# A reordered opening and 128-row attention scores in a two-layer streaming encoder

## The chip, the cores and the metric

The kernel runs on one core of a Trainium2 chip. The metric is the time of one execution on the device in microseconds. Engines in the rows: PE is TensorE (matmuls), PEld its weight loads, DVE is VectorE, ACT is ScalarE, POOL is GpSimd and SP is the engine whose queue issues nearly all DMAs.

## What is computed

512 frames of width 1024 pass through two layers; all data is float32.

```python
h = rms_norm(x, ev_norm_g)                       # layer 0
z = h @ w_in                                     # 1024 -> 2560: u_a, gate_a, val_b, glu_b, gate_b
y_a = s5_mixer(u_a, ...) * silu(gate_a)          # 32 groups of 16 channels, 64 complex states each
y_b = conv_module(val_b, glu_b, ...) * silu(gate_b)   # GLU, causal depthwise conv of 31 taps, LayerNorm, SiLU
x = x + concat(y_a, y_b) @ w_out
x = x + mem_cross_attention(rms_norm(x), mem_n, ...)  # 4 heads, 256 memory tokens
h = rms_norm(x, od_norm_g)                       # layer 1
q, k, v, g = split(h @ w_in, 4)                  # 16 heads of 64
s = q @ k.T * scale + bias                       # chunks of 64; each sees itself and 8 before it
x = x + (softmax(s) @ v * silu(g)) @ w_out
x = x + mem_cross_attention(rms_norm(x), mem_n, ...)
return rms_norm(x, final_norm_g)
```

`s5_mixer` discretises a diagonal complex system (exp, sine and cosine of the parameters), runs it as a scan over the frames, and ends in a GELU and a gated linear unit (GLU).

## The kernel before

Activations stand channel-major: eight tiles of 128 channels x 512 frames. Precision is kept by splitting each f32 operand into a rounded high half and a low half; a projection tile `proj` of 128 output channels is 24 matmuls of 512 columns (high x high, high x low, low x high over eight input tiles). Its weights come through `weights`: DMA into `raw` (three buffers), high half on ScalarE into `whi` (two buffers), low half by a subtraction on GpSimd or, if asked, VectorE into `wlo` (three buffers). The result goes to a PSUM buffer `proj`, of which there are three.

The scheduler orders each engine's queue from the traced order, priorities and its own model of times; what is marked `pinned` stays behind what was traced before it on its engine. Each queue then runs in that order.

Layer 0 begins with loads and splits written out by hand (`LOADS`, `ACTS`): ScalarE makes high halves of `h`, squares for the norm follow, VectorE makes low halves and adds the squares. TensorE warms up, runs the first two tiles (u0, u1) as the tiles of x come in (`first_mm`), then tile w12 in parts, with the row sums (`st0.done`, four one-column f32 matmuls) pinned between its first twelve matmuls and the rest. `rsqrt` on VectorE turns the sums into the norm, a matmul broadcasts it over the partitions, and ScalarE copies it to `rb0`: every tile's result is multiplied by `rb0` as it leaves PSUM.

`s5_tables` follows: some 150 small VectorE operations that make the discretised system and the rotation tables. Then the stage runs in the order of `PLAN`; each letter is a step for tile or slice i:

- u: S5 input tile (`state_input`), with a round trip through DRAM. c: gate tile and value tile of the conv (`conv_input`). v: the conv as 40 small f32 matmuls (`conv_taps`). g: a gate tile.
- a, b, o: the S5 slice's tables (`s5_prep`), scan (`s5_scan`) and output (`s5_output`); y then goes through DRAM. The slices share the tiles `w`, `M` and `hh`.
- m, n: squares and sums of the memory. l, s: LayerNorm of the conv.

After the plan come the Gelu of each slice, the GLU's 16 f32 matmuls (line 891), the keys and values of the memory, the output projection, the first cross-attention, the chunk attention and the second cross-attention.

In the chunk attention, head pairs run through `score`, softmax, `transposed` and `weigh` with a written order, every matmul pinned; projection matmuls of later head pairs (`Filler`) lie between. A head's scores are two products: the tile `q` holds high and low half on 64 rows each, and the key's high half stands twice, so the first product has 128 rows; the second, q's high half with the key's low half, takes the 64 rows of that head:

```python
r = slice(64 * (hd % 2), 64 * (hd % 2) + 64)
terms=((q, k[hd % 2]), (q[r], k[2][r]))
```

Of the kernel before, what the change touches and what calls it, by code (L numbers as in the profile page):

```python
# [44 lines left out]
def kernel(  # L45
# [22 lines left out]
    V, A, G, T = nc.vector, nc.scalar, nc.gpsimd, nc.tensor  # L68
# [133 lines left out]
    class Stats:  # L202
# [13 lines left out]
        def done(self, scale=1.0 / D, pin=False):  # L216
            nb = self.n // P
            ps = psum("acc")
            for b in range(nb):
                c = slice(b * P, (b + 1) * P)  # L220
                ins = T.matmul(ps[:, b:b + 1], self.acc[:, c], ones[:, 0:1], start=True, stop=(self.late is None))
                if pin:
                    pinned(ins)
# [47 lines left out]
    def s5_tables(l0):  # L271
# [13 lines left out]
        def exp16(out, a):  # L285
            a = ts(slot(), a, -87.33, 88.37, ALU.max, ALU.min)
# [60 lines left out]
        run(exp16(dt, pc("log_dt")))  # L347
# [109 lines left out]
        cp = l0.tile([P, 2, NPAIR, 32], F32, name="cp")  # L457
        pinned(G.memset(cp, 0.0))
# [17 lines left out]
        w = [l0.tile([P, 4, 4, 32], F32, name=f"w{e}") for e in range(4)]  # L476
        M = l0.tile([P, 4, 4, 32], F32, name="M")
        for t in w + [M]:
            pinned(G.memset(t, 0.0))
        hh = [l0.tile([P, 4, NJ], F32, name=f"hh{e}") for e in range(2)]  # L480
        d3 = l0.tile([P, 4, NJ], F32, name="d3")
        for t in hh + [d3]:
            pinned(G.memset(t[:, :, 0:1], 0.0))
        return dict(pr=pr[:, :, 1:5], npi=npi, apr=ap[0], api=ap[1], rot=rot, far=ang[:, 8], m4=m4,
                    bb=wide(bb), cz=wide(cz), cp=cp, w=w, M=M, hh=hh, d3=d3)
# [40 lines left out]
    def s5_scan(tb, sl, U, prep):  # L526
# [13 lines left out]
        powers(qs, tb["pr"], tb["npi"], tb["cz"], w2r, w2i, ALU.add, ALU.subtract, True, G, "g")  # L540
# [148 lines left out]
    N12 = 12  # L689
    WLO = 'VVVV'  # L690
# [21 lines left out]
    with tc.high_priority():  # L712
        for job in ACTS.split():
            n = int(job[1])
            if job[0] == "x":
                ins = A.activation(h0[n][0], x[n], AF.Copy, scale=pc("ev_g", n))
                stt(h0[n][1], x[n], pc("ev_g", n), f(h0[n][0]), ALU.mult, ALU.subtract)
# [9 lines left out]
            else:  # L727
                c = slice(0, 4) if job[0] == "a" else slice(4, 8)
                ins = A.copy(his[job], raws[n][:, c])
                tt(los[n][:, c], raws[n][:, c], f(his[job]), ALU.subtract,  # L730
                   {"G": G, "V": V}[WLO[2 * (job[0] == "b") + n]])
            pinned(ins)
# [20 lines left out]
    w12 = weights(w_in_d[12])  # L753
    ps12 = psum("proj")
    mm12 = [(w12[i][:, k], h0[k][j]) for i, j in ((0, 0), (0, 1), (1, 0)) for k in range(KT)]

    def run12(lo, hi, pin=False):
        for n in range(lo, hi):
            ins = T.matmul(ps12, mm12[n][0], mm12[n][1], start=(n == 0), stop=(n == len(mm12) - 1))
            if pin:  # L760
                pinned(ins)
# [10 lines left out]
    def conv_input(i):  # L772
        ps = proj(weights(w_in_d[12 + i], eng=V if UENG[4 + 2 * i] == "V" else G), h0) if i else ps12
# [4 lines left out]
        ps = proj(weights(w_in_d[8 + i], eng=V if UENG[5 + 2 * i] == "V" else G), h0)  # L778
# [725 lines left out]
```

## Time and profile before

| | us |
|---|---|
| median of three runs (1022.0, 1023.16, 1024.18) | 1023.16 |
| profiled execution | 1018.19 |
| its span, first to last instruction | 1016.4 |
| TensorE busy in the span | 975.5 |
| VectorE, ScalarE, GpSimd busy | 565.1, 467.3, 453.1 |
| mean granted TensorE clock, of full speed | 0.979 |

Times in rows are microseconds from the start of the span. Busy time of TensorE counts a pipelined matmul from its start to a modelled end, so records overlap; the distance from one start to the next is what a matmul takes in a run of them. Each f32 matmul stands as two records. "idle before <-releaser" is what the engine waited for.

### The profile page before, as it was taken

The numbers are of one execution on the slowest core, as the hardware profiler recorded it, in microseconds if no ns is written. First come the engines' busy times: TensorE is split into PE (matmuls) and PEld (weight loads), VectorE is DVE, ScalarE is ACT, GpSimd is POOL, SyncE is SP. The second block draws the span as 40 slices with busy tenths as digits, with TensorE's granted clock in tenths as the row PEclk, the third lists the DMA queues.
The fourth block names the chain that finished last, engine by engine and source line by source line (L and its number), as shares of the span: only waits on it lengthen the run. The fifth ranks groups of instructions, "written<-read, shape, count | busy, mean of one in ns | idle before, by whom it ended". The sixth has DMA issues, their size and how long they took to land.

```text
span 1016.4 us, 14244 instructions
## 1 busy us (share of the span) xinstructions
PE 975.5 (96%) x5336; PEld 825.6 (81%) x5336; DVE 565.1 (56%) x1249; ACT 467.3 (46%) x844; POOL 453.1 (45%) x252
## 2 busy tenths in 40 slices
PE   8979999998999999999999999999999999999996
PEld 6768998867978888888778787787878898888895
DVE  8895665454144433353477677767667412333476
ACT  6223444364444433344355555556645543333352
POOL 2530332016857434437443345335426885344242
PEclk9987999999999999999999999999999999999998
DMA  7455556535532222223222122221213453222153
GB/s 256 134 149 174 152 173 188 156 104 185 189 124 84 83 83 65 80 68 109 84 77 69 63 94 70 76 68 68 75 62 109 143 183 116 84 83 63 62 165 106
DMA packets 53620, 113.71 MB, mean 112 GB/s; under 512 B 13232, under 2 KB 24624, under 8 KB 53552
## 3 DMA queue, kind: packets, MB, share of 16 engines
q1 hardware_dynamic: 53408, 112.74, 34.9%
q8 instruction: 42, 0.69, 0.3%
q14 instruction: 26, 0.21, 0.1%
q10 hardware_dynamic: 144, 0.07, 0.0%
HBM read 106.50 MB, written 6.29 MB: 111 GB/s over the span
## 4 chain that ended last, share of the span: by engine, by line
PE 38%; DVE 7%; issue 2%; ACT 2%; POOL 1%; DMA 1%; POOLq 0%; ACTq 0%; DVEq 0%
PE ps_proj L978 20%; PE ps_proj L175 4%; PE ps_proj L1170 3%; PE ps_proj L630 2%; PE ps_att L1213 2%; PE ps_tr L1243 2%; PE ps_att L1040 1%; PE ps_acc L1256 1%; PE ps_tr L1256 1%; DVE h L139 1%; ACT whi L150 1%; DVE pe L144 1%; POOL wlo L135 1%; DVE o L135 1%; DVE tz L144 1%
## 5 line engine op out<-in xcount | busy, mean ns | idle before, releaser
L135 POOL TENSOR_TENSOR wlo<-raw,whi 128x1024 fp32r<-128x1024 f32 x133 | 322.2, 2425 | 416.0 <-ACT whi L150 394.0
L150 ACT CAST whi<-raw 128x1024 fp32r<-128x1024 f32 x148 | 154.9, 1048 | 194.4 <-issue 52.5
L978 PE MATMUL ps_proj<-h,whi 128*128 128x512 f32 x896 | 228.6, 398 | 0.0
L978 PEld LDWEIGHTS ps_proj<-h,whi 128*128 128x128 f32 x896 | 164.3, 189 | 36.8 <-issue 4.1
L978 PE MATMUL ps_proj<-h,wlo 128*128 128x512 f32 x448 | 115.6, 397 | 0.0
L175 PE MATMUL ps_proj<-og,whi 128*128 128x512 f32 (+1 forms) x576 | 109.8, 340 | 0.6 <-DVE og L135 0.6
L175 PEld LDWEIGHTS ps_proj<-og,whi 128*128 128x128 f32 x576 | 90.0, 188 | 14.3 <-DVE og L135 2.0
L978 PEld LDWEIGHTS ps_proj<-h,wlo 128*128 128x128 f32 x448 | 85.0, 191 | 18.4 <-issue 0.2
L175 PE MATMUL ps_proj<-h,whi 128*128 128x512 f32 x272 | 71.6, 410 | 1.6 <-ACT whi L150 1.6
L175 PEld LDWEIGHTS ps_proj<-h,whi 128*128 128x128 f32 x272 | 51.5, 195 | 13.4 <-ACT whi L150 2.1
L135 DVE TENSOR_TENSOR pt<-ps_tr,pt 128x512 fp32r<-128x512 f32 (+1 forms) x80 | 39.9, 525 | 33.0 <-ACT pt L150 32.8
L175 PE MATMUL ps_proj<-og,wlo 128*128 128x512 f32 (+1 forms) x288 | 57.9, 338 | 0.0
L150 ACT CAST pt<-ps_tr 128x512 fp32r<-128x512 f32 (+1 forms) x80 | 34.2, 460 | 46.8 <-PE ps_tr L1243 28.2
L139 DVE SCALAR_TENSOR_TENSOR h<-x,par,h 128x512 fp32r<-128x512 f32 x32 | 47.0, 1474 | 13.5 <-ACT h L229 13.5
L1222 ACT ACTIVATE pe<-ps_att,s 128x128 f32<-128x128 f32 (+3 forms) x64 | 33.5, 525 | 39.4 <-DVE s L144 34.3
L135 POOL TENSOR_TENSOR sa<-sa,sq 128x512 f32<-128x512 f32 (+1 forms) x28 | 39.0, 1392 | 27.5 <-ACT sq L210 27.3
L175 PEld LDWEIGHTS ps_proj<-og,wlo 128*128 128x128 f32 x288 | 45.7, 188 | 6.4 <-POOL wlo L135 0.2
L144 DVE TENSOR_SCALAR pe<-pe,s 128x256 f32<-128x256 f32 (+3 forms) x96 | 50.0, 543 | 1.4
L135 DVE TENSOR_TENSOR kv<-ps_proj,kv 128x256 fp32r<-128x256 f32 (+1 forms) x24 | 12.2, 510 | 68.8 <-ACT kv L150 68.8
L794 PEld LDWEIGHTS ps_proj<-x,cw 128*128 128x128 f32 x320 | 44.3, 215 | 6.0 <-DVE uu L135 3.5
L794 PE MATMUL ps_proj<-x,cw 128*128 128x64 f32 (+4 forms) x320 | 45.0, 297 | 3.8 <-DVE uu L135 3.1
L135 DVE TENSOR_TENSOR z<-ps_proj,rb 128x512 f32<-128x512 f32 x32 | 22.0, 687 | 47.2 <-PE ps_proj L978 47.1
(256 smaller groups left out, 1643.3 us busy)
## 6 DMA issues: line engine op xcount, KB each, us to landing
raw<-in_xa_qg_dram SPq DMA_DIRECT2D x32, 512.0 KB, 3.5
raw<-in_od_qkg_dram SPq DMA_DIRECT2D x24, 512.0 KB, 3.5
raw<-in_xa_o_dram SPq DMA_DIRECT2D x22, 512.0 KB, 3.5
cw<-in_cw_dram SPq DMA_DIRECT2D x32, 320.0 KB, 3.1
raw<-in_w_in_dram SPq DMA_DIRECT2D x18, 512.0 KB, 4.0
raw<-in_xa_k_dram SPq DMA_DIRECT2D x16, 512.0 KB, 3.5
raw<-in_xa_v_dram SPq DMA_DIRECT2D x16, 512.0 KB, 3.5
x<-in_xT_dram SPq DMA_DIRECT2D x16, 256.0 KB, 4.6
```

Source lines behind the costliest of these rows:

```text
L135: (eng or V).tensor_tensor(out, a, b, op=op)
L139: V.scalar_tensor_tensor(out=out, in0=a, scalar=s, in1=b, op0=op0, op1=op1)
L144: V.tensor_scalar(out=out, in0=in0, scalar1=s1, scalar2=None, op0=op0)
L150: A.copy(hi, src)
L175: T.matmul(ps, a, b, start=(i == 0), stop=(i == len(prods) - 1))
L630: T.matmul(o, a[:, ts_], b[:, k, :], start=(e == 0 and low == 0 and t % 2 == 0 and k == 0 and j == 0), stop=(e == 1 and low == 1 and t % 2 ...
L794: T.matmul(ps[:, q * CJ + d:(q + 1) * CJ], w[:, d, :], vb[i][:, q, :CJ - d], start=(d == 0), stop=(d == CB - 1))
L978: pinned(T.matmul(ps, a, b[:, cols], start=(i == 0), stop=(last is None and i == len(prods) - 1)))
L1170: pinned(T.matmul(o, a[:, ts_], b[:, k, :], start=(e == 0 and low == 0 and t % 2 == 0 and k == 0 and j == 0), stop=(e == 1 and low == 1 an ...
L1213: pinned(T.matmul(ps[:, c:c + n], a[:, sl], b[:, :n], start=(j == 0), stop=(j == 1)))
L1222: A.activation(st_["pe"][i], ps[:, c:c + n], AF.Exp, bias=nb, accum_out=st_["sums"][:, i:i + 1])
L1243: pinned(T.transpose(ps[:, (i - j) * P:(i - j + 1) * P], st["pe"][i][:, j * P:(j + 1) * P], ident))
```

## The change

The first matmuls are pinned through a wrapper around TensorE's calls, until the third projection tile has been traced. The order is now: u0, u1, w12 and w8, row sums, w2, broadcast of the norm. GpSimd's memsets for the S5 stage (`s5_fixed`) are traced before the first loads. `s5_tables` is traced as a step `t0` of the plan, behind the first quarter of v0, and its first operations must issue behind the last low half of `h`. `conv_input` is split into z (gate tile) and c (value tile), `conv_taps` runs in quarters of two of eight blocks, and the plan is new. The low halves of w12, and of the tiles up to g0, are made on VectorE, as are the z products of tiles 0 and 1 and the second powers of slice 0; the squares of the memory are pinned on ScalarE. In the chunk attention the key's low half gets two tiles, each with zeros on the other head's 64 rows (four memsets on GpSimd), so that the second product has 128 rows as well; one tile more of 128 x 512 is allocated (`kl`).

```diff
+    class TensorEngine:
+        ordered = True
+        def keep(self, ins):
+            if self.ordered:
+                tc.keep_in_program_order(ins)
+            return ins
...
+    def s5_fixed(l0):
+        cp = l0.tile([P, 2, NPAIR, 32], F32, name="cp")
+        G.memset(cp, 0.0)
+        w = [l0.tile([P, 4, 4, 32], F32, name=f"w{e}") for e in range(4)]
+        M = l0.tile([P, 4, 4, 32], F32, name="M")
+        for t in w + [M]:
+            G.memset(t, 0.0)
...
-    def s5_tables(l0):
+    def s5_tables(l0, fixed, after):
...
-        run(exp16(dt, pc("log_dt")))
+        with tc.issue_after(after):
+            run(exp16(dt, pc("log_dt")))
...
-        powers(qs, tb["pr"], tb["npi"], tb["cz"], w2r, w2i, ALU.add, ALU.subtract, True, G, "g")
+        powers(qs, tb["pr"], tb["npi"], tb["cz"], w2r, w2i, ALU.add, ALU.subtract, True, G if sl else V, "g")
...
-            st.add(t)
+            st.add(t, pin=True)
...
-    PLAN = "u0 u1 c0 u2 u3 c1 v0 g0 a0 b0 m0 o0 a1 v1 b1 c2 o1 g1 a2 n0 b2 v2 o2 c3 g2 a3 b3 v3 o3 g3 g4 l0 s0 g5 g6 g7"
-    UENG = 'VVVVVVVVGGVG'
-    GATE_V = (3, 5, 7)
+    PLAN = "u0 u1 z0 c0 u2 u3 z1 c1 g0 v0 t0 g1 v0 v0 v0 a0 z2 b0 c2 v1 v1 v1 v1 g2 o0 a1 z3 b1 c3 v2 v2 v2 v2 g3 o1 a2 m0 g4 b2 v3 v3 v3 v3 g5 o2 a3 b3 n0 g6 l0 s0 o3 g7"
+    UENG = 'VVVVVVVVVVGG'
+    GATE_V = (0, 3, 5, 7)
...
+    fixed = s5_fixed(l0)
     raws = [tl("raw", (P, KT, P)) for _ in range(2)]
...
-            pinned(ins)
+            if job[0] not in "gv":
+                pinned(ins)
...
-    w12 = weights(w_in_d[12])
-    ps12 = psum("proj")
...
-    run12(0, N12, True)
+    first_c = [proj(weights(w_in_d[n], eng=V), h0) for n in (12, 8)]
     with tc.high_priority():
-        rs0 = st0.done(pin=True)
-    run12(N12, len(mm12))
+        rs0 = st0.done()
+    third = proj(weights(w_in_d[2], eng=V), h0)
     with tc.high_priority():
         rb0 = rb_tile(rs0)
-    tb = s5_tables(l0)
+    T.ordered = False
...
+    def conv_gate(i):
...
-            tt(z, z, rb0, ALU.mult, G)
+            tt(z, z, rb0, ALU.mult, V if i < 2 else G)
...
-        ps = psum("proj")
-        for q in range(8):
+        if taps.get(i) is None:
+            taps[i] = [psum("proj"), 0]
+        ps, q0 = taps[i]
+        for q in (q0, q0 + 1):
...
-                        lo = rl("sq")
+                        lo = klo[hp % 2]
                         tt(t, ps, norm["rb"], ALU.mult)
-                        split(t[u], a[u], lo[u], QE[2])
-                        split(t[d], b[d], lo[d], QE[3])
+                        split(t[u], a[u], lo[0][u], QE[2])
+                        split(t[d], b[d], lo[1][d], QE[3])
...
+            klo.extend([(rl("sq"), rl("sq")), (rl("kl"), rl("sa"))])
+            for pair in klo:
+                for e, t in enumerate(pair):
+                    G.memset(f(t[64 * (1 - e):64 * (2 - e)]), 0.0)
...
-            r = slice(64 * (hd % 2), 64 * (hd % 2) + 64)
...
-            return dict(terms=((q, k[hd % 2]), (q[r], k[2][r])), tz=tz, mx=small(), sums=small(), inv=small(), pe=[])
+            return dict(terms=((q, k[hd % 2]), (q, k[2 + hd % 2])), tz=tz, mx=small(), sums=small(), inv=small(), pe=[])
```

## Rows read from the trace of the kernel before

**Rows 1.** The page's first part: busy time of each engine, share of the span, instructions.
```profile
PE 975.5 (96%) x5336; PEld 825.6 (81%) x5336; DVE 565.1 (56%) x1249; ACT 467.3 (46%) x844; POOL 453.1 (45%) x252
```

**Rows 2.** Busy time by stage: stretch, its length, busy time of each engine (records), granted TensorE clock, DMA share, GB/s.
```profile
0.00:28.00 28.00, 22.27 (x83) 17.73 (x83) 23.78 (x81) 16.59 (x27) 6.80 (x17) 1.00 0.69 237
28.00:48.00 20.00, 19.39 (x80) 15.65 (x81) 15.58 (x70) 7.18 (x12) 10.99 (x11) 0.91 0.36 119
48.00:79.00 31.00, 24.90 (x103) 20.10 (x102) 27.07 (x54) 7.93 (x15) 11.86 (x10) 0.89 0.59 178
79.00:104.00 25.00, 23.33 (x151) 22.89 (x150) 15.03 (x32) 8.71 (x22) 3.82 (x4) 0.73 0.52 153
240.00:252.00 12.00, 8.59 (x61) 8.20 (x60) 4.73 (x5) 3.76 (x5) 8.08 (x4) 0.86 0.78 251
500.00:760.00 260.00, 248.95 (x1366) 202.55 (x1365) 184.45 (x516) 144.94 (x317) 105.56 (x54) 0.99 0.22 72
```

**Rows 3.** The same columns (PE, PEld, DVE, ACT, POOL, clock, DMA) for three stretches of the opening.
```profile
30.91:34.31 3.40, 3.40 (x9) 2.63 (x9) 3.36 (x17) 1.74 (x5) 1.14 (x1) 0.50 0.36 106
68.45:75.27 6.82, 6.82 (x27) 6.24 (x28) 6.62 (x7) 1.56 (x2) 4.21 (x3) 0.50 0.83 251
88.93:102.58 13.65, 12.89 (x61) 12.71 (x61) 8.12 (x14) 2.62 (x8) 0.25 (x1) 0.50 0.54 161
```

**Rows 4.** What TensorE waited for up to 104: waiting matmul, releaser, us in total, times, longest.
```profile
PE ps_proj L794 <- DVE uu L135: 3.1, 1, 3.1
PE ps_att L740 <- DVE h L139: 2.6, 1, 2.6
...
PE ps_proj L175 <- ACT whi L150: 1.6, 1, 1.6
PE ps_proj L175 <- DVE wlo L135: 1.4, 1, 1.4
...
PE ps_att L740 <- DVE s L135: 1.0, 1, 1.0
```

**Rows 5.** Instructions of VectorE and GpSimd in order of time: start, duration, engine, line, operation, output<-input, shapes, count.
```profile
14.68 2.62 POOL L135 TENSOR_TENSOR wlo<-raw,whi 128x1024 fp32r<-128x1024 f32 x1 [13.28 <-ACT whi L150]
...
14.95 5.72 DVE L144 TENSOR_SCALAR s<-s 128x16 f32<-128x16 f32 x1
...
18.13 1.93 POOL L479 MEMSET w<- 128x512 f32 x4
...
66.61 0.68 DVE L135 TENSOR_TENSOR m<-pw,bz 128x512 f32<-128x512 f32 x1
```

**Rows 6.** TensorE's matmuls of the opening in order of time, the same columns; runs of like ones are merged, and the last one's duration is in the merged time.
```profile
21.55 2.01 PE L740 MATMUL ps_att<-h,wlo 128*128 128x512 f32 x8
...
28.61 1.02 PE L221 MATMUL ps_acc<-ones,gate 128*128 128x1 f32 x8 [1.65 <-DVE s L135]
...
45.05 3.79 PE L175 MATMUL ps_proj<-h,whi 128*128 128x512 f32 x16
48.68 1.98 PE L175 MATMUL ps_proj<-h,wlo 128*128 128x512 f32 x8
...
79.37 1.03 PE L512 MATMUL ps_tr<-ident,w 128*128 128x128 f32 x8
...
111.31 1.22 PE L794 MATMUL ps_proj<-x,cw 128*128 128x64 f32 x10
```

**Rows 7.** VectorE in the opening, in order of time: a low half of weights, the first two products with rb.
```profile
25.05 1.22 DVE L135 TENSOR_TENSOR wlo<-raw,whi 128x1024 fp32r<-128x1024 f32 x1
...
37.92 1.10 DVE L135 TENSOR_TENSOR uu<-ps_att,rb 128x512 f32<-128x512 f32 x1
38.86 0.69 DVE L135 TENSOR_TENSOR ev<-ps_proj,rb 128x512 f32<-128x512 f32 x1
```

**Rows 8.** The end of the S5 stage in order of time: the last copy of y, the product that reads it after its way through DRAM, the GLU's matmuls.
```profile
190.19 0.58 ACT L586 COPY y<-ps_att 128x512 f32<-128x512 f32 x1 [0.36 <-PE ps_att L584]
...
204.13 0.74 DVE L139 SCALAR_TENSOR_TENSOR uu<-uu,par,y 128x512 f32<-128x512 f32 x1
...
214.61 13.89 PE L891 MATMUL ps_proj<-uu,raw 128*128 128x512 f32 x32
```

**Rows 9.** TensorE's matmuls in the three score blocks of the second head pair, in order of time, with what follows each; 64*128 are the products on 64 rows.
```profile
538.82 0.33 PE L1213 MATMUL ps_att<-qk,qk 128*128 128x128 f32 x2
...
540.09 0.72 PE L978 MATMUL ps_proj<-h,whi 128*128 128x512 f32 x2
...
544.97 0.57 PE L1213 MATMUL ps_att<-qk,qk 128*128 128x384 f32 x2
...
545.84 1.45 PE L978 MATMUL ps_proj<-h,whi 128*128 128x512 f32 x5
...
549.87 0.61 PE L1213 MATMUL ps_att<-qk,qk 128*128 128x512 f32 x2
550.41 0.50 PE L1213 MATMUL ps_att<-sq,qk 64*128 64x512 f32 x2
550.84 1.40 PE L978 MATMUL ps_proj<-h,whi 128*128 128x512 f32 x5
```

**Rows 10.** Runs of matmuls of 256 columns (scores of the cross-attention) and of 128 columns (transposes) on 128 rows.
```profile
425.67 1.57 PE L1040 MATMUL ps_att<-kv,q 128*128 128x256 f32 x12
...
532.35 0.93 PE L1243 MATMUL ps_tr<-ident,pe 128*128 128x128 f32 x7
```

More of the change, by code (lines that the diff above doesn't have):

```diff
@@ L67, with matmul, transpose @@
     nc = tc.nc
-    V, A, G, T = nc.vector, nc.scalar, nc.gpsimd, nc.tensor
+    V, A, G = nc.vector, nc.scalar, nc.gpsimd
+    class TensorEngine:
[4 more added lines that the diff above has]
+            return ins
+        def matmul(self, *args, **kw):
+            return self.keep(nc.tensor.matmul(*args, **kw))
+        def transpose(self, *args):
+            return self.keep(nc.tensor.transpose(*args))
+    T = TensorEngine()
     uid = [0]
@@ L214, in add, with done @@
                 tt(self.acc, self.acc, s, ALU.add, eng or G)
-        def done(self, scale=1.0 / D, pin=False):
+        def done(self, scale=1.0 / D):
             nb = self.n // P
@@ L220, in done @@
                 c = slice(b * P, (b + 1) * P)
-                ins = T.matmul(ps[:, b:b + 1], self.acc[:, c], ones[:, 0:1], start=True, stop=(self.late is None))
-                if pin:
-                    pinned(ins)
+                T.matmul(ps[:, b:b + 1], self.acc[:, c], ones[:, 0:1], start=True, stop=(self.late is None))
                 if self.late is not None:
@@ L269 @@
     BIASED = RND + 127.0
-    def s5_tables(l0):
+    def s5_fixed(l0):
[5 more added lines that the diff above has]
+            G.memset(t, 0.0)
+        hh = [l0.tile([P, 4, NJ], F32, name=f"hh{e}") for e in range(2)]
+        d3 = l0.tile([P, 4, NJ], F32, name="d3")
+        for t in hh + [d3]:
+            G.memset(t[:, :, 0:1], 0.0)
+        return dict(cp=cp, w=w, M=M, hh=hh, d3=d3)
+    def s5_tables(l0, fixed, after):
         def slot(n=1):
@@ L283, in horner, with exp16 @@
             return acc
-        def exp16(out, a):
-            a = ts(slot(), a, -87.33, 88.37, ALU.max, ALU.min)
+        def exp16(out, x):
+            a = slot()
+            ts(a, x, -87.33, 88.37, ALU.max, ALU.min)
             yield
@@ L456, in s5_tables @@
         nc.sync.dma_start(cz, s5c_d)
-        cp = l0.tile([P, 2, NPAIR, 32], F32, name="cp")
-        pinned(G.memset(cp, 0.0))
+        cp = fixed["cp"]
         for g in range(2):
@@ L474, in s5_tables @@
         run(table())
[L476 to L483, printed above, removed]
         return dict(pr=pr[:, :, 1:5], npi=npi, apr=ap[0], api=ap[1], rot=rot, far=ang[:, 8], m4=m4,
-                    bb=wide(bb), cz=wide(cz), cp=cp, w=w, M=M, hh=hh, d3=d3)
+                    bb=wide(bb), cz=wide(cz), **fixed)
     qslice = [slice(4 * i, 4 * i + 4) for i in range(4)]
@@ L752, with tables @@
             first_mm(n, j, 2)
-    w12 = weights(w_in_d[12])
-    ps12 = psum("proj")
[L755 to L761, printed above, removed]
-    run12(0, N12, True)
+    first_c = [proj(weights(w_in_d[n], eng=V), h0) for n in (12, 8)]
     with tc.high_priority():
-        rs0 = st0.done(pin=True)
-    run12(N12, len(mm12))
+        rs0 = st0.done()
+    third = proj(weights(w_in_d[2], eng=V), h0)
     with tc.high_priority():
         rb0 = rb_tile(rs0)
-    tb = s5_tables(l0)
-    def conv_input(i):
-        ps = proj(weights(w_in_d[12 + i], eng=V if UENG[4 + 2 * i] == "V" else G), h0) if i else ps12
+    T.ordered = False
+    tb = {}
+    def tables(_):
+        tb.update(s5_tables(l0, fixed, last_lo))
+    def conv_gate(i):
+        ps = proj(weights(w_in_d[12 + i], eng=V if UENG[4 + 2 * i] == "V" else G), h0) if i else first_c[0]
         with tc.high_priority():
@@ L776, in conv_input @@
             A.activation(z, z, AF.Sigmoid)
[L777 to L778 removed]
+            tt(z, z, rb0, ALU.mult, V if i < 2 else G)
+        zc[i] = z
+    def conv_input(i):
+        z = zc[i]
+        ps = proj(weights(w_in_d[8 + i], eng=V if UENG[5 + 2 * i] == "V" else G), h0) if i else first_c[1]
         v = tl("x", (P, CP, CJ))
@@ L801, in conv_taps @@
         A.activation(conv[i], conv[i], AF.Identity, bias=pc("conv_b", i))
-    vb, conv = [None] * 4, [None] * 4
+    taps = {}
+    zc, vb, conv = [None] * 4, [None] * 4, [None] * 4
     uP, U, ys, gates = [None] * 4, [None] * 4, [], [None] * 8
     def state_input(i):
-        ps = proj(weights(w_in_d[i], eng=V if UENG[i] == "V" else G), h0) if i > 1 else first_ps[i]
+        ps = proj(weights(w_in_d[3], eng=V), h0) if i == 3 else third if i == 2 else first_ps[i]
         t = tl("uu", (P, 4, NJ))
@@ L860, in ln_scale @@
         lst.rs = lst.done(1.0 / 512)
-    stages = {"u": state_input, "c": conv_input, "a": prep, "b": scan, "o": out, "g": gate, "m": mem_sums, "n": mem_scale, "v": conv_taps,
-              "l": ln_centre, "s": ln_scale}
+    stages = {"u": state_input, "z": conv_gate, "c": conv_input, "a": prep, "b": scan, "o": out, "g": gate, "m": mem_sums, "n": mem_scale, "v": conv_taps,
+              "l": ln_centre, "s": ln_scale, "t": tables}
     for job in PLAN.split():
```

25 lines of the change are left out of this document (15 added, 10 removed).

## Prediction

> **What bounds the kernel now.** I read the page first: TensorE is busy for 975.5 us, 96% of the span [rows 1]. So time can be won in two ways only: TensorE has less to do, or its idle time and its time at the lower clock shrink. The table by stages says where those lie [rows 2]: length less busy time is 5.7 + 0.6 + 6.1 + 1.7 = 14.1 us of idle before 104, 3.4 at 240 to 252, 11.0 in the chunk attention (500 to 760); of the 40.9 us in all, little else is left before the last stage. The granted clock is below full in the same opening: 0.91, 0.89, 0.73. Its three stretches are at 0.50, which is 1.2 of 2.4 GHz, with 3.4, 6.8 and 12.9 us of matmul work in them [rows 3]. At half rate work takes twice its time, so they cost 1.7 + 3.4 + 6.4 = 11.5 us. What did TensorE do before each? A wait of 1.65 and one-column matmuls; a gap of 3.1; a run of small S5 and conv matmuls. The opening thus loses about 25 us, and the opening is what the change rewrites.
>
> The list of waits names what ended the gaps [rows 4]: mostly VectorE, which is busy for 23.8 of the first 28 us and 27.1 of 31 us from 48 to 79 [rows 2]. Why is it so full? One table operation on 16 columns is on it for 5.72 us from 14.95, while in just these microseconds GpSimd runs a 2.62 us subtraction and then its memsets [rows 5]. The last low half of h came behind that, and TensorE waited 1.0.
>
> **The change, part by part.** The sum is made against the profiled execution, 1018.19 us, 1.8 of it around the span.
>
> *First matmuls.* The table operations go behind the last low half of h, and GpSimd's memsets to the front, where VectorE still waits for its first data. So of the 2.6 wait for h [rows 4] 1.1 stays (the low half needs ScalarE's high half): gain 1.5, bounds 0 and 2.6. The wait of 1.0 goes. The first 48 matmuls ended at 23.6 [rows 6] and now end at 21.1.
>
> *Row sums behind four tiles.* A tile of 24 matmuls takes 5.45 (sixteen in 3.63, from 45.05 to 48.68) [rows 6]. With w12 and w8 ahead of the row sums, VectorE's adds have 10.9 us to hide behind; the wait of 1.65 goes, and with it, I hold, the half-rate stretch at 30.9 (1.7). But the change adds a wait here. All three projection buffers (w12, w8, w2) are full when rb comes, and its broadcast is pinned behind w2. Tile u3 gets a buffer only after broadcast, ScalarE's copy of rb (0.58, as y's [rows 8]) and VectorE's products, 1.10 for uu and 0.69 for ev [rows 7]. In the old order this chain ran beside tiles; now TensorE idles for 0.6 + 1.1 + 0.7 = 2.4, or 3.5 if both uu go first: I take 2.9.
>
> *Tables late, low halves on VectorE.* The waits of 1.6, 1.4 and 3.1 [rows 4] and the half rate behind them (3.4) came from a VectorE queue full of stalled table operations. After: 21.1 + 10.9 + row sums 1.0 + w2 5.45 + broadcast 0.9 (two records at 13.89/32 [rows 8]) + gap 2.9 = 42.3; then u3, z1, c1 and g0 to 64.1, a quarter of v0 to 66.3 (ten records 1.22 with the last one's tail, so about 2.2 for twenty) [rows 6]. In the old trace the same work ended at 79.4: 13.1 ahead. The ledger of waits agrees: 1.5 + 1.0 + 1.65 + 1.6 + 1.4 + 3.1 + half rate 1.7 + 3.4 - 2.9 = 12.5, which I use.
>
> Can VectorE follow? To 66.6, where its old tables ended [rows 5], it was busy for 58 us (23.8 + 15.6 + a full 18.6 [rows 2]). To the first powers it gets on top: low halves of w12 and w4 (1.22 each), two z products (0.69), the four evictions that came later (two of 1.10, two of 0.69) and the powers (two of 0.68 and four smaller, some 2.8): 68. Without the 5.0 us that the long stall cost, and a second one of 2, 61. Beginning at 4.4 it ends between 65 and 72. TensorE wants a0 behind g1 and v0's other quarters, 66.3 + 5.45 + 6.6 = 78. Hidden, with 6 to 13 to spare; beyond that each us costs one, once z2 and c2 are used up. Slice 0's second powers also move to VectorE, off TensorE's path: the scan is before them.
>
> *Conv in quarters.* From 79 to 104 the old order ran conv and S5 matmuls alone, at half rate: 6.4 + 1.7 idle [rows 2, 3]. With quarters between 512-column tiles this can go wholly or not at all: 0 to 8.1. I take 4.0, because v0's last three quarters, a0 and b0 still stand close together.
>
> *Memory and S5 end.* The eight loads of mem, ScalarE's squares (now pinned) and GpSimd's adds move behind a2; they are wanted by n0, a slice later, so I cost them at nothing. If SP's queue held them back, l0, which shares their tile, would wait. Behind o3 five gate tiles stood, now one. y goes through DRAM: from its copy at 190.19 to the product at 204.13 and the Gelu, 14.5 us [rows 8]. g7 covers 5.45 of that and the GLU's three open sums (of 13.9, nine sixteenths do not need slice 3) 7.8. I charge 2, bounds 0 and 6. For a half-rate stretch behind the 2.9 gap I charge 1.0, bounds 0 and 3.4.
>
> Opening: 12.5 + 4.0 - 2.0 - 1.0 = 13.5.
>
> *Scores on 128 rows.* Per pair of heads the old blocks take 1.27 (538.82 to 540.09), 0.87 (544.97 to 545.84) and 0.97 (549.87 to 550.84) = 3.11 [rows 9]. The 64-row matmuls of the two heads do overlap: two of 512 columns occupy 0.43, from 550.41 on. But that is hardly less than two full ones in sequence, and each change of the row count leaves a gap. On 128 rows all are ordinary matmuls: 0.227 for 512 columns; 0.118 to 0.131 for 256 and 0.097 to 0.133 for 128 (twelve in 1.57, seven in 0.93, the upper with the tail of the last) [rows 6, 10]; 0.172 between for 384. Four of each: 2.46 to 2.65, a saving of 0.46 to 0.65, eight times: 3.7 to 5.2. TensorE is busy for 249 of 260 us there [rows 2]; in the other 11 it waits for chains of VectorE and ScalarE that get no faster, so part of the saving may be waited away: 0 to 5.2, I take 4.2. GpSimd's four memsets of 512 columns (0.5 each [rows 5]) lie beside two projection tiles; uncovered, they would delay one low half by 2.
>
> The Trainium skill, page "TensorEngine Tiling", section "When to Use Tiling", speaks against this part: a contraction over 64 belongs in two row tiles, up to twice as fast. By that rule widening would lose 4.5 in place of the 4.2 gained. The rows bear out the overlap but not the gain; the page's "Key Properties" also say that a change of tiling mode drains the engine.
>
> Total: 13.5 + 4.2 = 17.7: 1000.5 for the profiled execution. The median of the runs shown lies 5.0 above it, at 1023.16, so I forecast 1005.5, say 1005.
>
> **The rivals.**
> 1. *The low halves starve (slower).* VectorE's queue is in order and now carries GpSimd's low halves too, so one may stand behind table operations. Such waits cost 1.6, 1.4 and 3.1 [rows 4], mean 2.0, and 1.7 at half rate behind each. With one at each of u3, z1, c1, g0, g1, z2, c2 and g2: 8 x 3.7 = 30, less 17.7: 12 slower, 1035. It decides from the fifth tile. For it: VectorE is full already. Against it: the stalls beside GpSimd leave the queue.
> 2. *The opening's gain is eaten where it arises.* Half rate behind the rb gap (3.4), conv still at half rate, 6 behind o3: 12.5 - 9.4 = 3.1, with the scores 7.3: 1016.
> 3. *Row tiling was worth it.* If the paired 64-row matmuls run at half price, widening adds 1280 columns per pair of heads, 0.57 x 8 = 4.5: 13.5 - 4.5 = 9.0, 1014. Against it: the 0.43 for two of them. This is the page's rule.
> 4. *Nothing arrives.* The time saved is waited for later, as at 240 to 252, where the DMA share is 0.78 and TensorE idles 3.4 [rows 2]: 1022.
>
> **How the numbers follow.** Forecast 0.57 (own range 997 to 1012), starving 0.10, eaten 0.17, row tiling 0.08, nothing 0.08. The range leaves out starving and nothing: from the forecast with upper bounds (8.1 for conv, no tail, no stretch, 5.2 for the scores: 8 more, and some 3 for a clock that rises earlier in the first matmuls) to a little above rival 2: 994 to 1019. A measurement of this kernel tells 0.2%, 2 us, from no change. Faster 0.82, same 0.08, slower 0.10.
>
> **What would show it.** Right: no table operation on VectorE before the last low half of h; the first 48 matmuls ended by 21; no wait for the row sums; one gap of 2.4 to 3.5 behind the broadcast, then none over 1 until a0; a0's transposes near 78 with g1 done; at most one half-rate stretch between 30 and 104; score blocks all on 128 rows, of 0.86 to 1.05, 0.69 and 0.91. Wrong: TensorE waiting for low halves after 42, a0 later than 82, a gap of over 3 between o3 and the GLU, or longer waits of the attention's transposes.

## The result and the profile after

The changed kernel takes 997.3 us (median, 994.67 to 998.8) beside 1022.58 us for the kernel before: a ratio of 0.975, 95% interval 0.972 to 0.978. A repeat gave 0.976 (0.973 to 0.979). The direction and the range of the prediction held; the forecast of 1005 was 8 us too high. The profiled execution of after took 994.67 us, 23.5 less than that of before, where the sum had promised 17.7.

Busy time by stage, in the columns of [rows 2] (104 to 240 is added):

```profile
0.00:28.00 28.00, 25.53 (x102) 20.80 (x103) 20.75 (x71) 17.69 (x28) 4.20 (x16) 0.94 0.77 264
28.00:48.00 20.00, 17.64 (x80) 14.06 (x79) 20.00 (x113) 6.38 (x8) 0.00 (x0) 1.00 0.37 127
48.00:79.00 31.00, 31.00 (x168) 26.64 (x167) 19.74 (x37) 10.08 (x16) 6.11 (x3) 1.00 0.68 198
79.00:104.00 25.00, 23.38 (x155) 20.82 (x154) 14.65 (x22) 11.15 (x22) 8.45 (x4) 1.00 0.56 163
104.00:240.00 136.00, 130.27 (x813) 110.40 (x813) 86.97 (x136) 70.68 (x129) 52.47 (x40) 1.00 0.56 170
240.00:252.00 12.00, 12.00 (x107) 12.00 (x106) 1.97 (x4) 6.39 (x9) 10.73 (x6) 1.00 0.60 197
500.00:760.00 260.00, 248.94 (x1398) 211.65 (x1397) 190.52 (x496) 145.36 (x311) 112.02 (x56) 0.99 0.23 76
```

Read the clock first: 1.00 in every stretch from 28 to 252, where it was 0.91, 0.89, 0.73 and 0.86. GpSimd runs nothing from 28 to 48 (11 us before). From 48 to 79 TensorE is busy throughout. New idle time stands at 104 to 240: 5.7 us (0.6 before).

What TensorE waited for up to 104, as in [rows 4]:

```profile
PE ps_proj L81 <- DVE ang L153: 2.4, 1, 2.4
PE ps_proj L81 <- DMA cw<-in_cw_dram: 1.6, 1, 1.6
PE ps_acc L81 <- POOL ones L137: 1.1, 1, 1.1
PE ps_att L81 <- ACT h L739: 0.8, 2, 0.6
PE ps_att L81 <- DVE h L740: 0.6, 2, 0.3
```

Up to 104 no tile waits for a low half any more. TensorE's matmuls in order of time, as in [rows 6, 8]:

```profile
20.30 3.79 PE L81 MATMUL ps_proj<-h,whi 128*128 128x512 f32 x16
...
31.18 0.95 PE L81 MATMUL ps_acc<-ones,gate 128*128 128x1 f32 x8
...
40.96 3.92 PE L81 MATMUL ps_proj<-h,whi 128*128 128x512 f32 x16 [2.36 <-DVE ang L153]
...
62.85 2.33 PE L81 MATMUL ps_proj<-x,cw 128*128 128x64 f32 x20
...
70.57 1.04 PE L84 MATMUL ps_tr<-ident,w 128*128 128x128 f32 x8
...
192.43 5.31 PE L81 MATMUL ps_proj<-uu,raw 128*128 128x512 f32 x12
...
205.37 5.40 PE L81 MATMUL ps_proj<-uu,raw 128*128 128x512 f32 x16 [1.15 <-ACT og L168]
212.55 3.72 PE L81 MATMUL ps_proj<-uu,raw 128*128 128x256 f32 x16 [1.79 <-ACT uu L641]
```

The first 48 matmuls are over at 20.30; the row sums (31.18) wait for nothing; behind the broadcast comes one gap of 2.36, then u3 at 40.96; a0's transposes begin at 70.57, in place of 79.37.

Where the time went, by landmarks of TensorE in the two profiled executions (us): the last native key matmul begins at 221.9, before 239.3 (17.4 earlier); the first cross-attention scores start 19.5 earlier, so the K/V stage gave 2.1 more; the chunk scores still 19.5; the chunk attention's last product with v 23.8; TensorE's last matmul 23.3.

**Time and clock apart.** Runs of one kernel differ by several us, largely with their mean granted clock (0.970 to 0.983 for the kernel before). So I also use time multiplied by mean clock: about what a run would take if all of it were at full clock, since TensorE is busy nearly throughout. The product is no exact measure: a half-rate stretch that lengthens nothing lowers it too.

| kernel (runs) | mean us | mean clock | time x clock, with standard error |
|---|---|---|---|
| before (43) | 1019.7 | 0.975 | 994.7 ± 0.3 |
| after (10) | 996.0 | 0.989 | 985.4 ± 0.4 |

Of the 23.7 us, by this measure, only 9.3 are less work and less waiting; 14.4 are clock.

### The profile page after: what moved, and what is told of

The parts are those of the page before. It is cut to its first block, busy times and chain, and to the rows that moved or that the text cites. A ratio compares the mean times of both kernels' runs of the same rounds, so it can differ in the third digit from the quotient of the medians.

```text
span 992.9 us, 14232 instructions
## 1 busy us (share of the span) xinstructions
PE 956.0 (96%) x5336; PEld 817.4 (82%) x5336; DVE 565.7 (57%) x1260; ACT 469.2 (47%) x845; POOL 442.3 (45%) x245
## 4 chain that ended last, share of the span: by engine, by line
PE 34%; DVE 9%; issue 3%; ACT 2%; DMA 1%; POOL 1%; POOLq 0%; ACTq 0%; DVEq 0%
PE ps_proj L81 27%; PE ps_att L81 2%; PE ps_tr L84 2%; PE ps_acc L81 2%; PE ps_tr L81 1%; DVE pe L162 1%; ACT whi L168 1%; DVE ps_att L1270 1%; DVE tz L162 1%; DVE o L153 1%; DVE h L157 1%; POOL wlo L153 1%; ACT pe L1257 1%; DVE s L1269 1%; DMA mt<-in_memT_dram 1%
## 5 line engine op out<-in xcount | busy, mean ns | idle before, releaser
L81 PE MATMUL ps_proj<-h,wlo 128*128 128x512 f32 x592 | 151.7, 394 | 0.0
L81 PE MATMUL ps_proj<-og,whi 128*128 128x512 f32 (+1 forms) x672 | 135.0, 348 | 0.5 <-DVE og L153 0.5
L81 PEld LDWEIGHTS ps_proj<-h,wlo 128*128 128x128 f32 x592 | 111.0, 189 | 22.7
L81 PEld LDWEIGHTS ps_proj<-og,whi 128*128 128x128 f32 x672 | 107.6, 188 | 17.9 <-DVE og L153 2.0
L81 PE MATMUL ps_proj<-og,wlo 128*128 128x512 f32 (+1 forms) x344 | 73.4, 348 | 0.1
L81 PEld LDWEIGHTS ps_proj<-og,wlo 128*128 128x128 f32 x344 | 56.1, 188 | 8.9 <-POOL wlo L153 0.4
L153 POOL TENSOR_TENSOR sa<-sa,sq 128x512 f32<-128x512 f32 (+1 forms) x28 | 38.9, 1388 | 18.9 <-ACT sq L228 18.2
L153 DVE TENSOR_TENSOR x<-ps_proj,x 128x512 f32<-128x512 f32 (+1 forms) x38 | 22.9, 603 | 41.7 <-PE ps_proj L81 41.7
L157 DVE SCALAR_TENSOR_TENSOR h<-x,par,h 128x512 fp32r<-128x512 f32 x24 | 38.6, 1613 | 13.5 <-ACT h L247 13.5
L84 PE MATMUL ps_tr<-ident,pe 128*128 128x128 f32 x224 | 35.9, 279 | 9.5 <-DVE pe L162 5.0
L84 PEld LDWEIGHTS ps_tr<-ident,pe 128*128 128x128 f32 x224 | 27.1, 142 | 18.7 <-DVE pe L162 6.7
```

The lines of the kernel that those rows point to most:

```text
L81: return self.keep(nc.tensor.matmul(*args, **kw))
L84: return self.keep(nc.tensor.transpose(*args))
L153: (eng or V).tensor_tensor(out, a, b, op=op)
L157: V.scalar_tensor_tensor(out=out, in0=a, scalar=s, in1=b, op0=op0, op1=op1)
```

## The experiments

Times below are means; where a landmark is given it is from the run's profile.

**Scores alone, and all but the scores.** In the one, the kernel before gets the scores' part of the diff; in the other it is taken out of the changed kernel:

```diff
-            return dict(terms=((q, k[hd % 2]), (q[r], k[2][r])), ...
+            return dict(terms=((q, k[hd % 2]), (q, k[2 + hd % 2])), ...
```

> The kernel before with one part of the change alone: the scores' products of the low half of k on 128 rows, zeros in the other head's rows; the opening is untouched. My account: a pair of heads costs 2.58 us in score blocks in place of 3.11, as in the changed kernel's trace (0.92, 0.75 and 0.91 for 1.27, 0.86 and 0.98), eight pairs 4.2, and nothing of it is waited away at once: the chunk attention's stretch of 256.4 us shrinks to about 252, the run is 4 us (0.4%) faster. Rival, row tiling was worth it: the blocks get longer by 0.57 a pair, the run is 4.5 slower. Rival, the part brings nothing without the opening (the blocks are shorter, but TensorE waits for VectorE's exponent chain instead): the score blocks sum to 23.4 in place of 27.3 and the idle time of the stage rises by 4; no change.

> The changed kernel with the scores' low products back on 64 rows; everything else as changed. My account: the opening alone makes the gain of 19.5 us that is there when the chunk scores begin, so this kernel lies 4 us above the changed one and about 19 to 20 below the kernel before; the chunk attention lasts 256 us again and its score blocks 3.11 a pair. Rival: if the waits of the transposes that grew with the shorter blocks (7.7 to 9.3 us over the stage) fall back, only 2 to 3 us come back. Rival, row tiling: this one is faster than the changed kernel.

| | mean us | clock | time x clock |
|---|---|---|---|
| before with scores on 128 rows (9) | 1012.4 | 0.979 | 991.2 ± 0.5 |
| after with scores on 64 rows (6) | 1000.5 | 0.989 | 988.9 ± 0.5 |

The part is worth 3.5 either way at full clock (994.7 to 991.2; 988.9 to 985.4), so it brings the same with the new opening and without it. Row tiling loses. (The ratio of the first, 0.993, 0.991 to 0.996, is more than its share: its clock happened to be higher, and its profile has no stretch at half rate in the chunk attention where that of before has two.) The score blocks sum to 23.5 in place of 27.3, and the stage's idle time rises from 9.3 to 11.7; that would leave 1.5. The rest is in a place that I had not looked at, the tile behind a block. From the trace of after, one block of three on 128 rows and what follows it, in the columns of [rows 9]:

```profile
525.62 0.57 PE L81 MATMUL ps_att<-qk,qk 128*128 128x384 f32 x2
526.03 0.34 PE L81 MATMUL ps_att<-kl,qk 128*128 128x384 f32 x1
526.20 0.34 PE L81 MATMUL ps_att<-sa,qk 128*128 128x384 f32 x1
526.38 1.32 PE L81 MATMUL ps_proj<-h,whi 128*128 128x512 f32 x5
```

Five tile matmuls take 1.32 here; behind a block that ends on 64 rows the same five took 1.45 [rows 9]. Record by record, the first of them occupies TensorE for 0.338 us behind 64 rows and 0.230 behind 128 (medians over the 21 blocks that have a 512-column matmul behind them; the other three have one of 256 columns, which loses as much): 0.11 for each of 24 blocks, 2.6 us.

**Fewer changes of the row count.** On 64 rows again, with the first block of a pair ordered 128, 64 in place of 128, 64, 128, 64:

```diff
-            for i in rows:
...
-                for j in range(2):
...
+            for j in range(2):
...
+                for i in rows:
...
```

> The changed kernel with the low products on 64 rows, but ordered by row count inside the first block of a pair: the four products on 128 rows of both row tiles first, then the four on 64 rows. The order 128, 64, 128, 64 of that block becomes 128, 64: two changes of the row count fewer a pair, nothing else. If changing the row count is what eats the gain of the overlap (the trace of before shows gaps of 0.15 to 0.4 us at the changes), the first block falls from 1.27 to between 0.9 and 1.1, that is 1.4 to 3 us over eight pairs, and the other two blocks stay at 0.86 and 0.98. Rival: the two heads' 64-row products do not run side by side in time at all; then the first block stays at 1.2 to 1.3.

```profile
521.41 0.62 PE L81 MATMUL ps_att<-qk,qk 128*128 128x128 f32 x4
521.96 0.50 PE L81 MATMUL ps_att<-sq,qk 64*128 64x128 f32 x4
522.39 1.90 PE L81 MATMUL ps_proj<-h,whi 128*128 128x512 f32 x7
```

The block takes 0.98 (521.41 to 522.39) in place of 1.27: two changes fewer, one each way, save 0.29, so one costs about 0.15. Time x clock falls by 1.5, to 987.5 ± 0.3. The overlap of the two heads is real, and its gain goes into the changes: one into the 64 rows and one out of them is still enough to lose to 128 rows throughout (0.92).

**GpSimd at work beside the tables, and silent in the old order.** In the first, the changed kernel gets back the memsets inside the table code, and w12's and g0's low halves, the z products and slice 0's second powers on GpSimd; in the second, the kernel before gets just the reverse (the diff is of the first; in the second GpSimd is not quite silent, for seven adds of the memory's squares stay on it, 7.7 us in all):

```diff
-    first_c = [proj(weights(w_in_d[n], eng=V), h0) for n in (12, 8)]
+    first_c = [proj(weights(w_in_d[n], eng=e_), h0) for n, e_ in ((12, G), (8, V))]
...
-        cp = fixed["cp"]
+        cp = l0.tile([P, 2, NPAIR, 32], F32, name="cp")
+        pinned(G.memset(cp, 0.0))
```

> The changed kernel with GpSimd at work beside the tables again: its memsets stand inside the table code, it makes the low halves of w12 and g0, the two z products and slice 0's second powers; the tables stay late as in the change. If VectorE's stalls beside GpSimd are what the opening suffered from, single table operations of 16 or 32 columns take 1 to 6 us in place of 0.1 to 0.2, the low halves that VectorE makes come late, TensorE waits 1 to 3 us at several tiles between 30 and 75, and the run is 4 to 10 us slower. If only the lateness of the tables counted, the time is that of the changed kernel, within 1 us, since VectorE has less to do.

> The kernel before with one part of the change alone: GpSimd's memsets at the very front, and the low halves of w12 and g0, the z products of c0 and c1 and slice 0's second powers on VectorE, so that GpSimd is silent beside the tables but for seven small adds of the memory's squares; order, plan, tables' place and scores are those of before. If the stalls beside GpSimd made the old opening's waits, the table operation of 5.72 us falls to 0.2, the wait of 1.0 for the fourth low half goes, and those of 1.6, 1.4 and 3.1 at the tiles shrink to under 1 each, since VectorE gets 5 to 7 us back for the 6.6 of work that it takes over; o3 ends 3 to 8 us earlier than at 189.9. If what counts is the order (tables late, other tiles between the row sums and the broadcast, projection tiles beside the conv), the waits come back at other places because VectorE has more to do, the half-rate stretches from 68 to 103 stay, and o3 ends within 2 us of 189.9.

| | mean us | clock | time x clock | o3 ends |
|---|---|---|---|---|
| after, GpSimd beside the tables (4) | 1006.2 | 0.982 | 988.4 ± 0.5 | 198.0 (after: 188.4) |
| before, GpSimd silent (6) | 1007.3 | 0.982 | 989.0 ± 0.4 | 178.3 (before: 189.9) |

This is the largest of the parts tried: it moves o3 by 9.6 us one way and 11.6 the other, half-rate stretches included, more than I expected of the second. How it works is seen in the first, VectorE and GpSimd in order of time (in the columns of [rows 5]):

```profile
14.46 2.41 POOL L153 TENSOR_TENSOR wlo<-raw,whi 128x1024 fp32r<-128x1024 f32 x1 [13.04 <-ACT whi L168]
...
14.53 2.37 DVE L162 TENSOR_SCALAR s<-s 128x16 f32<-128x16 f32 x1
...
33.85 1.10 POOL L153 TENSOR_TENSOR g<-pw,cz 128x512 f32<-128x512 f32 x1 [16.99 <-DVE s L157]
...
33.95 1.03 DVE L157 SCALAR_TENSOR_TENSOR s<-s,s 128x4 f32<-128x4 f32 x1
...
35.24 1.04 POOL L153 TENSOR_TENSOR g<-npi,cz 128x512 f32<-128x512 f32 x1 [0.29 <-DVE s L153]
...
35.26 1.06 DVE L157 SCALAR_TENSOR_TENSOR ang<-ang 128x16 f32<-128x16 f32 x1
```

Each of these three VectorE operations starts just behind a GpSimd one and lasts until that one ends (16.90 beside 16.87, 34.98 beside 34.95, 36.32 beside 36.28); its kind takes 0.15 to 0.17 elsewhere. The Trainium skill, page "SBUF — State Buffer", section "SBUF: two separate sides", calls this an exclusive lock on a shared port, held by whichever of the two starts first; the trace agrees. It holds GpSimd too: in the kernel before with GpSimd silent, one low half of weights took it 5.14 us from 59.52, beside a VectorE without a pause, and the next, at 69.77, took 2.35. It matters where a stall falls: the one at 33.95 is in the row sums' reciprocal root (128x4), and the one at 35.26 stands in the queue ahead of that chain's end. TensorE waits for the broadcast (second line), then for a projection buffer (first line; the changed kernel has 2.4 of this):

```profile
PE ps_proj L81 <- DVE m L153: 3.0, 1, 3.0
PE ps_acc L81 <- DVE ang L153: 2.7, 1, 2.7
```

Behind the wait for the broadcast the clock falls, to 0.50 from 38.7 to 48.9. In the kernel before with GpSimd silent, the waits of 1.6, 1.4 and 3.1 at the tiles are gone, and TensorE's list up to 104 is headed by

```profile
PE ps_att L745 <- DVE h L139: 3.5, 1, 3.5
PE ps_att L586 <- DVE m L135: 1.4, 1, 1.4
PE ps_acc L699 <- POOL ones L119: 1.1, 1, 1.1
PE ps_acc L199 <- DVE s L135: 1.0, 1, 1.0
```

that is, by what its early tables (first line) and early row sums (last) cost. Its a0 starts at 66.8, ahead of the changed kernel's, which has one tile more in front (g1). What it doesn't have is the clock of the changed one: 0.78 from 79 to 104.

**Tables early, GpSimd silent.**

```diff
-        with tc.issue_after(after):
-            run(exp16(dt, pc("log_dt")))
+        run(exp16(dt, pc("log_dt")))
...
-    tb = {}
+    tb = s5_tables(l0, fixed, last_lo)
...
-        tb.update(s5_tables(l0, fixed, last_lo))
+        pass
```

> The changed kernel with the table operations traced ahead of the plan and free to start before the last low half of h; GpSimd stays silent until they end. It tells the lateness of the tables from the silence of GpSimd. If what held VectorE in the old order was that it ran beside GpSimd, the table operations stay at 0.1 to 0.2 us each and only those that come ahead of a low half of h delay it: the wait for h grows by at most 1.5, no single table operation takes over 1 us, the tiles' low halves come in time, and the run is 0 to 2 us slower. If the place of the tables in VectorE's queue itself made the waits, those of the old order come back (1.0 at the fourth low half, 1.6, 1.4 and 3.1 at the tiles), 4 to 8 us slower, with a half-rate stretch.

```profile
PE ps_att L81 <- DVE h L739: 3.5, 1, 3.5
PE ps_proj L81 <- DVE ev L153: 2.4, 1, 2.4
PE ps_proj L81 <- DMA cw<-in_cw_dram: 1.6, 1, 1.6
```

The wait for h is 3.5 in place of 0.6, nearly twice the growth that I allowed, with half clock from 7.5 to 14.4; everything later is as in the changed kernel, and o3 ends 2.2 later. Mean 1000.9, time x clock 987.9 ± 1.1: late tables are worth some 2 us (2.2 by o3, 2.5 by the product), all of it in the first matmuls.

**Conv whole; and no projection tiles beside it.** The first new plan is that of the conv whole, the second that of the tiles moved away:

```diff
-    PLAN = "... c1 g0 v0 t0 g1 v0 v0 v0 a0 z2 b0 c2 v1 v1 v1 v1 g2 o0 a1 z3 ..."
+    PLAN = "... c1 g0 t0 g1 v0 v0 v0 v0 a0 z2 b0 c2 v1 v1 v1 v1 g2 o0 a1 z3 ..."
...
+    PLAN = "... c1 g0 v0 t0 g1 v0 v0 v0 a0 b0 v1 v1 v1 v1 o0 a1 z2 c2 g2 z3 ..."
```

> The changed kernel with the conv whole again: the one quarter of v0 that stands ahead of g1 goes back to the other three, behind g1 (the quarters of v1, v2 and v3 stand together in the changed order already). Theory one, the quarters keep TensorE's clock up: without them a stretch at half rate with 3 to 6 us of work comes back between 65 and 104, the run is 2 to 6 us slower. Theory two, what keeps it up is that projection tiles (z2, c2, g2) are traced beside the conv and are woven in between its matmuls: the clock stays full from 30 to 250, the run is within 1 us, and a0's transposes come 2.2 earlier, at about 68.4.

> The changed kernel with the three projection tiles z2, c2, g2 taken out from between slice 0's conv and S5 work and put behind a1, as the order before had it; the quarters stay as in the change. Theory two above (tiles woven in keep the clock up): TensorE runs conv and S5 matmuls alone from about 71 to 95, one or two stretches at half rate come back there (cost 1.7 to 6), and with them waits for the S5 chain of VectorE of some 1 to 2 us: 3 to 8 us slower in all. Rival (the quarters do it, or the clock has nothing to do with what TensorE runs here): full clock from 30 to 104, and at most 2 us of waits.

Conv whole: 985.8 ± 0.4 in time x clock, full clock from 42 to 250, as theory two has it; but a0 is at 69.9, since the scheduler still ran one quarter ahead of it, so TensorE's order hardly differs from that of after, and this run alone tests little (the mean time, 999.3 over 4 runs at a clock of 0.987, is above that of after; the product and the profile's span, 992.2 beside 992.9, agree with it). The tiles moved away: 1003.3, clock 0.983, time x clock 986.5 ± 0.2, so nearly all of the loss is clock; o3 8.7 later. One stretch of this kernel and then the same of after, in the columns of [rows 2]:

```profile
81.00:94.40 13.40, 12.00 (x54) 11.72 (x55) 6.64 (x13) 2.62 (x8) 0.00 (x0) 0.50 0.50 137
```

```profile
81.00:94.40 13.40, 13.40 (x95) 12.33 (x94) 9.19 (x13) 5.31 (x13) 4.62 (x3) 1.00 0.53 152
```

Without the tiles TensorE runs 54 matmuls in a stretch at 1.2 GHz, with them 95 at 2.4 GHz. So it is the place of the tiles that recovers the clock; quarters without them do not. How the tiles do it is open, for they do two things: they put 512-column matmuls between narrow ones, and they fill waits. Without them TensorE waits three times for the conv's weights, and the stretch at half rate, from 80.8 to 94.5, begins in the longest of these waits:

```profile
PE ps_proj L81 <- DMA cw<-in_cw_dram: 2.4, 3, 1.3
```

No run separates the two, and neither alone fits every trace. In after, a wait of 1.62 for the same weights, which ends at 101.12, has full clock behind it. In the kernel with GpSimd beside the tables the clock is at half from 79.7 to 86.5 behind such a wait of 2.0, and in that with three remedies (below) from 152.9 to 163.1 behind one of 0.8, both times with 512-column matmuls between the conv's.

**Row sums one tile earlier.**

```diff
-    first_c = [proj(weights(w_in_d[n], eng=V), h0) for n in (12, 8)]
+    first_c = [proj(weights(w_in_d[12], eng=V), h0)]
     with tc.high_priority():
         rs0 = st0.done()
-    third = proj(weights(w_in_d[2], eng=V), h0)
+    first_c.append(proj(weights(w_in_d[8], eng=V), h0))
     with tc.high_priority():
         rb0 = rb_tile(rs0)
+    third = proj(weights(w_in_d[2], eng=V), h0)
```

> The changed kernel with the row sums behind three tiles in place of four and their broadcast behind four in place of five: order w12, sums, w8, broadcast, w2, u3. My account of the gap: TensorE idles 2.36 us behind the broadcast only because all three projection buffers are full until rb comes; with w2 still to run behind the broadcast the gap is covered. VectorE's adds ended at 23.8 and the sums would start near 25.8, so no wait for them: 2.4 us gained up to a0, a0's transposes at about 68.2 in place of 70.6, and 2.4 at the end of the run. Rival: the tables or the low halves are what a0 and the tiles wait for next, so the 2.4 come back as waits on VectorE before 104, and the run is unchanged. Rival: the sums wait for the adds again, 0.5 to 1.7 us, with a stretch at half rate behind the wait, and it is 1 to 3 slower.

```profile
25.51 0.95 PE L81 MATMUL ps_acc<-ones,gate 128*128 128x1 f32 x8
26.32 3.93 PE L81 MATMUL ps_proj<-h,whi 128*128 128x512 f32 x16
...
31.91 1.02 PE L81 MATMUL ps_acc<-dg,ones 128*128 128x512 f32 x2
32.36 4.24 PE L81 MATMUL ps_proj<-h,whi 128*128 128x512 f32 x16
```

No bracket on any line: neither the sums nor the tiles wait, and o3 ends at 185.6 (188.4). a0 starts only at 69.9 because a second quarter of v0 now runs ahead of it. Time x clock 982.1 ± 0.3, 3.3 below after; the mean time is 994.5 ± 1.1 beside 996.0 ± 0.8, which the clock's scatter hides.

**The end of S5.** A repeat of after as the measure (995.4, time x clock 985.6 ± 0.6), the memory's scale broadcast early, and three remedies together:

```diff
         mem["rs"] = mem["st"].done()
         T.ordered = False
+        with tc.high_priority():
+            mem["rb"] = bcast(mem["rs"], MEM, "tr")
...
-        ps = psum("proj")
+        ps = psum("proj" if i < 3 else "att")
         for k in range(4):
             T.matmul(ps, w[:, k, :], zs[k], start=(k == 0), stop=(k == 3))
```

(The second hunk is the GLU's, in the kernel with three remedies alone.)

> The changed kernel once more, on the same chip and beside the same runs of the kernel before as the next two, as the measure for them: 995 to 1000 us, a ratio of 0.973 to 0.979 to the kernel before, and a time multiplied by the mean granted clock near 985 us.

> The changed kernel with the broadcast of the memory's scale made right behind its sums, into a transpose buffer of PSUM, in place of behind the layer norm's sums in the one buffer of that tag. It tests the wait of 1.8 us on ScalarE's scaled memory in front of the first native key tile, which the kernel before did not have. My account: the memory's normalisation became the late thing because the tiles that stood between o3 and the GLU have moved ahead of o3; with the broadcast some 8 us earlier (189 to 191 in place of 199) the 1.8 goes, and the last native key product ends 1 to 2 us earlier, near 220.5; what is left are the 1.15 on a PSUM buffer of the GLU and the waits for the first non-native weights. Rival: the next waits (0.5 and 1.4 at the first non-native key tile) grow by the same amount, since ScalarE's and GpSimd's weight halves set them; no change at 250.

> Three remedies together: the row sums behind three tiles (as in the run of that name), the early broadcast of the memory's scale (as in the run before this one), and the GLU's fourth tile in a score buffer of PSUM, so that it needn't wait for the first GLU tile's sigmoid (1.15 us in the changed kernel). Expected if the gains add: 2.8 at o3's end, 1.2 and 1.8 behind it, 5 to 6 us in all: time multiplied by clock near 979.5, the run itself 990 to 993, 3% below the kernel before. Rival: TensorE meets the weights of the K/V stage earlier than ScalarE and GpSimd have split them, and all behind the 2.8 is given back before 250: 982.

What the rival said of the end came, but by another way. No later landmark is earlier (the first cross-attention scores start at 320.95 in this trace as in that of after), yet the waits that grew are not the next ones: TensorE waits for the scaled memory itself longer, not shorter, and the clock falls behind it.

```profile
213.05 9.72 PE L81 MATMUL ps_proj<-uu,raw 128*128 128x256 f32 x36 [2.54 <-ACT uu L641]
...
214.00:217.40 3.40, 3.40 (x9) 2.70 (x8) 1.07 (x3) 3.35 (x6) 2.07 (x2) 0.50 0.69 225
```

Time 995.6, beside 995.4 for the repeat; time x clock 983.2 ± 0.4, which is 2.4 lower although no landmark moved, so a difference of this size in the product alone shows no gain. So it isn't the broadcast that makes the memory late; ScalarE is busy for 14.2 of 18 us from 204 to 222 there, and I take its queue to be what does, which no run has separated. The three together (994.8; 982.4 ± 0.8) are no better than the row sums alone: the gains don't add, as their rival had it.

## Why the prediction was right, and where its sizes were wrong

1. *First matmuls.* Ended at 20.3, forecast 21.1. The tables' place shows it (22.7 with early tables). GpSimd's silence was not needed here: with GpSimd at work beside late tables they ended at 18.2. The clock moves this end more than either: 20.3 has 3.4 us at half rate in it, and three traces of the same opening without that stretch have 17.8 to 18.0, which is what the range's 3 us stood for.
2. *Row sums behind four tiles, gap behind the broadcast.* No wait; a gap of 2.36 where 2.4 to 3.5 was forecast, from the full buffers, as one tile between shows (gap gone). Four tiles were one too many.
3. *Half clock behind that gap,* charged with 1.0. In the traces of after and of its repeat the gap is 2.36 and the clock stays full behind it; there the clock had been at half for 3.4 us in the first matmuls already. In three kernels with the same opening up to the gap (scores on 64 rows, conv whole, tiles moved) the first matmuls ran at full clock, the gap came to 2.8 to 3.2, and the clock fell to half behind it. The bounds 0 and 3.4 held.
4. *Tables late, low halves on VectorE.* No tile waited, and the ledger of waits was right. u3 came at 40.96 (42.3), the first quarter ended at 65.0 (66.3). VectorE was done with the first powers by 62.9, ahead of my 65 to 72, and nothing waited for them. The scheduler had put a0 in front of v0's other quarters, where I had read it behind them: 70.6, not 78. The cause that I named, stalls beside GpSimd, is the one that the runs confirm, in both directions.
5. *Conv in quarters: the step that failed.* I took 4.0 of 0 to 8.1, "because v0's last three quarters, a0 and b0 still stand close together". The clock came back wholly. I had read the closeness from the plan; in TensorE's queue the matmuls of z2 run between the last three quarters, and those of c2 and g2 behind them and beside v1 (from 71.36 on). With these three tiles moved away, and the quarters kept, half rate returns. Whether it is their width or the waits that they fill is not shown. There is one profile of the kernel without them, but its mean clock agrees: 0.983 over 4 runs, against 0.989 over 10 of after.
6. *Memory at nothing, S5 end at 2.* The memory cost 1.8 at its first use and the GLU's last tile 1.15: 2.9 where I had charged 2, and not for the reason given, since no wait is put down to y's way through DRAM. That the 2 lay near is luck. Behind that the first split key tile cost 0.5 and 1.4, where the old order waited 3.4 at 240 [rows 2]; with the stretch at half rate that is gone there, this belongs to the K/V stage's further 2.1, which was in no term.
7. *Scores.* 4.2 forecast, 3.5 found. The blocks shrank as computed (0.53 a pair, forecast 0.46 to 0.65), the waits took back 2.4 of the 3.8 by which all blocks shrank, and the dearer matmul behind each block, which [rows 9] already showed as 1.45 and 1.40 for five, gave 2.6: some 4 by the records, 3.5 by the runs. That the matmul behind the block, which I left out, made up for the waits is luck too.

Sum it by kind. Of the 17.7, the half-rate terms (1.7 + 3.4 + 4.0 - 1.0, with conv counted whole as clock) are 8.1, waits and scores 9.6. Measured: clock 14.4, the rest 9.3. So the waits and the work came out well as a sum, in which errors of single terms cancel (points 6 and 7), and the error of the total is the clock: up to 252 the trace of before has 27.3 us at half rate ([rows 3] and a stretch of 3.4 behind the waits at 240), which cost 13.7; that of after has 3.4, in the first matmuls, which cost 1.7. I had let half of the conv's share stay and had charged a new one, and left out the one at 240. These 12.0 are from one trace of each kernel, and the clock has scatter: the trace of before with 128-row scores has 34.1 us at half rate up to 252, with the opening unchanged. The other 2.4 of the 14.4 are not traced.

The rivals: no tile starved; the opening's gain was not eaten; row tiling was not worth it; what was saved in the opening did arrive, though some of what the later remedies saved did not.

## What to carry to other kernels

Count the time at half clock as a term of its own and ask of each such stretch what TensorE ran in it and what it had waited for just before: here three projection tiles placed beside the conv were worth 7.3 us, more than any one shortened wait. Take the order from the queue, not from the traced plan. Keep GpSimd off while VectorE runs chains of short operations that others wait for; with two stalls of 1 us there TensorE waited 5.7 us, where it waited 2.4 without them, and then ran 10 us at half clock. And when a matmul shape is changed, price the matmul behind it too.

## What the hardware showed that I had not expected

- A change of the row count costs about 0.15 us inside a block (two fewer save 0.29), and the first full matmul behind a block that ends on 64 rows takes 0.11 more (0.338 against 0.230). The Trainium skill, page "TensorEngine Tiling (Array Packing)", section "When to Use Tiling", gives two row tiles for a contraction over 64; here they lose 3.5 us over 8 pairs of heads. The drain that its section "Key Properties" states fits the changes that were measured.
- GpSimd's operations in a row held VectorE for the whole row: the table operation of 5.72 us [rows 5] started inside GpSimd's subtraction and ended, at 20.67, with the memsets behind that.
- Runs of one kernel differ in mean granted clock by over a hundredth, which is 10 us here, so a remedy of 3 us shows in the product of time and clock (982.1 ± 0.3 against 985.4 ± 0.4) and hardly in the time. It wants a landmark beside it: there o3 ended 2.8 earlier; with the memory's early broadcast the product fell by 2.4 and no landmark behind it was earlier.
